# State space products in neighbouring column and row groups, and norm sums taken tile by tile, in a two-block fp32 kernel

## The chip, the cores and the metric

One NeuronCore of a Trainium2 chip. The metric is device microseconds of one execution. Of the engines, PE is TensorE (matmul), DVE VectorE, ACT ScalarE, POOL GpSimd; SP is the engine whose queue issues most DMAs. L12 is line 12 of the kernel before.

## The reference, cut to what matters

Two blocks in a row on x of 512 tokens by 1024, all in fp32; a context of 256 tokens goes into the first.

```python
# block 1 (m = the six modulation vectors, from silu(c) @ w_mod + b_mod)
hc = _modulate(ctx, g_norm1, m_c[0], m_c[1])
hx = _modulate(x, g_norm1, m_x[:, 0], m_x[:, 1])          # rms norm, * (1 + scale) + shift
x = x + m_x[:, 2] * _mixer_out(hx @ w_in, yx_lru, ...)    # RG-LRU and chunk branches, w_out
h2 = _modulate(x, g_norm2, m_x[:, 3], m_x[:, 4])
x = x + m_x[:, 5] * _conv_ffn(h2, w_up, ffn_conv_w, ffn_conv_b, w_down, rows, GRID_W)
x = _rmsnorm(x, g_final)
# block 2
h = rms_norm(x, mix_norm_g)
u, q, k, v, f_logit, g_ssm, g_att = jnp.split(h @ w_in, IN_SPLITS, axis=-1)
y_ssm = s5_branch(u, ...)              # 32 groups: x = B u, complex scan, y = Re(C s) + d u, glu
y_att = forgetting_attention(q, k, v, f_logit, ...)       # q and k normed by head
x = x + (sigmoid(g_ssm) * y_ssm + sigmoid(g_att) * y_att) @ w_out
x = x + peer_ffn(rms_norm(x, ffn_norm_g), w_query, sub_keys, peer_u, peer_v)
```

## The kernel before, in words

Activations lie transposed: 128 channels on the partitions, 8 tiles k (KT), 512 tokens (T) along the free axis; the context has 256 (TC). For fp32 accuracy every large product is three matmuls, hi by hi, hi by lo and lo by hi (mm3, L121 to 124). The halves are made by a pair of operations: ACT copies a value rounded to fp32r, DVE subtracts it from the value (weights whi and wlo, L114 and L115; activations, split_to, L142 to 145). Weights come in pieces of 512 KB over SP's queue into four raw buffers; whi and wlo have three buffers each. proj (L131) makes one column of 128 outputs from eight k, 24 matmuls, and get_w loads and splits a column's weights, once, at the first call. The build orders the instructions of each engine by a list scheduler from their readiness and their program order; every engine then runs its list in order.

Stages, in us from the span's start: opening 0 to 63; RG-LRU 63 to 302 (lru_in, lru_gates, v_cols); chunk branch, gates and w_out to 638; norm 2 to 672; conv FFN to 1026; final norms to 1062; attention with the state space between its parts to 1420; w2_glu and w2_out to 1563; norm 3 to 1590; then the expert layer (query, top 16, peer_u, peer_v) to 2891.

**Norms.** A norm over channels is a sum over the partitions and the eight k. ACT squares all eight tiles, colsum (L147) adds them in PSUM by eight matmuls against ones in four column groups of 32, ACT copies the result, and tok_mean (L154) brings it to tokens on partitions by one small matmul for each 128 tokens. rstd_of (L164) is the root (whose first use loads a table on ACT) and a reciprocal; bcast_tok (L170) spreads it over the partitions by four diagonal copies and four matmuls; scaled_split (L180) makes each normed tile (nt, hi, lo).

**Modulation.** A chapter of w_mod is 512 columns: mod_a (L203) runs eight fp32 matmuls in four column groups and copies the result, mod_b (L215) transposes it and adds the bias. Chapters 0 and 1 are the shift, 2 and 3 the scale of norm 1, 10 and 11 the factor behind the FFN.

**Opening (L237 to 285).** SP issues x, ctx and the four chapters, 2 MB each, in wm, which has two buffers. Both norms, the four chapters in order, then eight steps k of h tiles for x and for ctx; the projections of w_rx column 0 and then 1 (lru_in, L330) use them, in PSUM pool ps1 with four banks of the tag mm; ps2 has two double banks.

**Chunk branch.** v_w (L403) loads a quarter of w_v. **w_out (L674 to 677)** and **w_down (ffn_down, L793; last calls L817)** update x1 column by column; **norm 2 (L735 to 755)** has mod_a of chapters 10 and 11 in it; the **final norms (L832 to 856)** form mean1 of x1, mean2 of x1*gf and r1, r2, write x1*gf*r1 back (L854) and make hb.

**Attention and S5 (L862 to 1181).** s5_step (L1006) is put 17 times between the parts of attention. Step s runs s5_y of s-1 and s5_x of s, s from 0 to 15. s5_x (L969) has two matmuls over 32 rows, L974 real and L975 imaginary, both in row group s mod 4, into two banks, and 12 DVE operations on 128x512: six that multiply by the factors e from DRAM, two scans, four products sr, p, w2, w1. s5_y (L996) has four matmuls (L1002) of 32 output columns into column group s mod 4 of one bank, py; after each fourth step DVE adds d*u. fp32 matmuls appear as two instructions each. a_sums (L1033) sums squares of two of q, q, k, k in column groups; a_norm1 (L1035) is root and reciprocal; a_norm2 (L1041) spreads rows of rs by four matmuls (L1045), each with its own full selq and a bank of its own. All share eight banks (psD).

**w2_out (L1218 to 1221), norm 3 (L1257 to 1260)**: then rows_of_x3 (L1263) transposes token tiles of x3; the order is tile NTD = 3, 0, 1, 2.

The core of the places where the order is set by hand, before:

```python
for ch in range(4):                                   # opening
    mod_b(psp, s[ch], ch)
    if ch < 2:
        s.append(mod_a(psp, wk, ch + 2, whole=wm[ch + 2]))
def s5_step():
    s = S5["n"]
    if s > 16:
        return
    if s > 0:
        s5_y(s - 1)
    if s < 16:
        s5_x(s)
    if s < 15:
        s5_e(s + 1)
```

Of the kernel before, what the change touches and what calls it, by code (L numbers as in the profile page):

```python
# [21 lines left out]
T = 512  # L22
# [50 lines left out]
def tile_kernel(ctx: ExitStack, tc: tile.TileContext, I, out, dump=None, stop=None):  # L73
# [22 lines left out]
    c32 = const.tile([128, 2], F32, name="c32")  # L96
    nc.vector.memset(c32, 1.0 / (32 * D))
# [49 lines left out]
    def colsum(ps, sqs, n):  # L147
        K = len(sqs)
        for k in range(K):
            g = k % 4  # L150
            nc.tensor.matmul(ps[32 * g:32 * g + 32, :n], ones[:, :32], sqs[k], start=k < 4, stop=k >= K - 4)  # L151

    def tok_mean(wk, psp, sqs, n, tag):

        pa = psp.tile([128, 512], F32, name="pa", tag="mm")
        colsum(pa, sqs, n)
        s = wk.tile([128, n], F32, name="ssum", tag="ssum", bufs=1)
        nc.scalar.activation(s, pa[:, :n], AF.Copy)
        pb = psp.tile([128, 512], F32, name="pb", tag="mm")
        for t in range(n // 128):  # L160
            nc.tensor.matmul(pb[:, 2 * t:2 * t + 2], s[:, t * 128:(t + 1) * 128], c32, start=True, stop=True)
        return pb[:, 0:2 * (n // 128):2]
# [52 lines left out]
    def mod_b(psp, s, ch):  # L215
        pt = psp.tile([128, 512], F32, name="pt", tag="mm")
# [23 lines left out]
    wm = []  # L240
    for ch in range(4):
        t = wk.tile([128, 8, 512], F32, name="wm", tag="wm", bufs=2)
        for q in range(2):
            nc.sync.dma_start(t[:, 4 * q:4 * q + 4], I["w_mod"][ch][:, 4 * q:4 * q + 4])
        wm.append(t)

    def sq_of(src, n):
        s = wk.tile([128, n], F32, name="sq", tag="sq", bufs=4)
        nc.scalar.activation(s, src, AF.Square)
        return s  # L250
# [1451 lines left out]
```

## Time and profile before

| what | value |
|---|---|
| median of 3 runs | 2893.77 us (2893.13 to 2897.28) |
| profiled execution | 2892.62 us |
| its span in the profile | 2890.8 us |
| DVE, ACT, POOL busy | 73%, 40%, 17% of the span |
| HBM traffic | 186 GB/s over the span |

A row of a timeline has start and duration in us, engine, line, operation, output and inputs by the program's names, shapes and count; in brackets the idle time of the engine before it and what ended it. Durations of PE overlap, since matmuls are pipelined: what one costs is read from start to start.

### The profile page before, as it was taken

To read this page: it belongs to the slowest core of one execution; us is meant where nothing else is said; L and a number is where in the kernel's file an instruction comes from. 1 tells how busy PE (TensorE), PEld (TensorE's weight loads), DVE (VectorE), ACT (ScalarE), POOL (GpSimd) and SP (SyncE) were. 2 spreads that over 40 slices of the span, in tenths; PEclk is the share of its full clock that TensorE was granted. 3 is DMA by queue.
4 is the path that set the end of the run, shared out by engine and by line. 5 is a ranking of instruction groups with operands and counts; after the bars stand their busy time and mean duration, and the time that the engine had idled before them with its cause. 6 is when DMAs were issued, how large, how long until landed. Compare 5 with 4: busy or idle time off the path is not lost.

```text
span 2890.8 us, 37068 instructions
## 1 busy us (share of the span) xinstructions
PE 2785.8 (96%) x13917; PEld 2280.5 (79%) x13917; DVE 2099.1 (73%) x3645; ACT 1159.4 (40%) x1599; POOL 492.2 (17%) x452
## 2 busy tenths in 40 slices
PE   7999999999999999999999988999998989999999
PEld 5777888877888866656687888898998978777887
DVE  5786894339777665777544999999785579988554
ACT  4667523224333343333433334555553333333332
POOL 0000000000000000000000016546343357652000
PEclk8999999999999999999999999999999999999999
DMA  6333263333333332222233237898899699999663
GB/s 246 122 112 109 97 196 106 124 114 105 97 92 96 89 124 73 73 73 66 75 102 116 88 126 267 299 340 310 323 330 337 234 349 380 401 390 347 216 214 116
DMA packets 167476, 540.11 MB, mean 187 GB/s; under 512 B 16896, under 2 KB 42112, under 8 KB 163840
## 3 DMA queue, kind: packets, MB, share of 16 engines
q1 hardware_dynamic: 128128, 391.94, 39.7%
q0 software_dynamic: 36864, 134.23, 12.5%
q10 hardware_dynamic: 2304, 11.57, 1.1%
q8 instruction: 109, 1.79, 0.2%
q14 instruction: 71, 0.58, 0.1%
HBM read 479.48 MB, written 58.20 MB: 186 GB/s over the span
## 4 chain that ended last, share of the span: by engine, by line
PE 74%; DVE 10%; issue 6%; DMA 5%; POOL 3%; ACT 3%; SPq 0%; DVEq 0%; POOLq 0%; ACTq 0%
PE pmm L122 15%; PE pmm L124 15%; PE pmm L123 15%; PE acc L1604 13%; DMA raw<-in_peer_v_rows_dram 3%; DVE wlo L115 2%; PE pmm L1002 2%; POOL rows L1458 2%; DVE rows L1471 1%; PE pm L209 1%; PE pa L151 1%; POOL rows L1457 1%; PE pg L122 1%; PE pg L123 1%; ACT whi L114 1%
## 5 line engine op out<-in xcount | busy, mean ns | idle before, releaser
L114 ACT ACTIVATE whi<-raw 128x1024 fp32r<-128x1024 f32 (+2 forms) x502 | 518.1, 1033 | 1023.3 <-PE pmm L123 773.4
L115 DVE TENSOR_TENSOR wlo<-raw,whi 128x1024 fp32r<-128x1024 f32 (+2 forms) x502 | 608.0, 1212 | 283.5 <-ACT whi L114 278.9
L124 PE MATMUL pmm<-nph,wlo 128*128 128x384 f32 (+1 forms) x1152 | 398.9, 347 | 20.3 <-DVE wlo L115 20.2
L122 PE MATMUL pmm<-nph,whi 128*128 128x384 f32 (+1 forms) x1152 | 405.7, 352 | 0.3 <-ACT whi L114 0.3
L123 PE MATMUL pmm<-npl,whi 128*128 128x384 f32 (+1 forms) x1152 | 397.5, 345 | 0.0
L1604 PE MATMUL acc<-whi,wth 128*128 128x512 f32 x768 | 243.0, 397 | 7.3 <-ACT whi L114 7.3
L1604 PE MATMUL acc<-wlo,wth 128*128 128x512 f32 x768 | 243.6, 398 | 6.2 <-DVE wlo L115 6.1
L124 PEld LDWEIGHTS pmm<-nph,wlo 128*128 128x128 f32 x1152 | 220.3, 191 | 29.9 <-DVE wlo L115 24.8
L1604 PE MATMUL acc<-whi,wtl 128*128 128x512 f32 x768 | 242.6, 397 | 0.0
L122 PEld LDWEIGHTS pmm<-nph,whi 128*128 128x128 f32 x1152 | 220.6, 192 | 5.1 <-ACT whi L114 0.6
L123 PEld LDWEIGHTS pmm<-npl,whi 128*128 128x128 f32 x1152 | 220.4, 191 | 4.5
L1458 POOL DMA_INDIRECT rows<-in_peer_v_rows_dram,idx x128 | 202.0, 1578 | 108.5 <-DVE accN L1486 97.5
L1471 DVE SCALAR_TENSOR_TENSOR rows<-rows,hN 128x1024 f32<-128x1024 f32 x128 | 155.1, 1218 | 55.3 <-DMA rows<-in_peer_u_rows_dram,idx 55.3
L1486 DVE SCALAR_TENSOR_TENSOR accN<-rows,dot,accN 128x1024 f32<-128x1024 f32 x128 | 163.7, 1279 | 27.3 <-DMA rows<-in_peer_v_rows_dram,idx 27.0
L1604 PEld LDWEIGHTS acc<-wlo,wth 128*128 128x128 f32 x768 | 143.8, 188 | 45.8 <-DVE wlo L115 11.0
L1604 PEld LDWEIGHTS acc<-whi,wth 128*128 128x128 f32 x768 | 144.6, 189 | 44.3 <-ACT whi L114 9.2
L1604 PEld LDWEIGHTS acc<-whi,wtl 128*128 128x128 f32 x768 | 144.8, 189 | 35.8
L1458 POOL DMA_INDIRECT rows<-in_peer_u_rows_dram,idx x128 | 164.0, 1281 | 48.6 <-POOL rows L1457 26.0
L144 ACT ACTIVATE wth<-w 128x384 fp32r<-128x384 f32 x128 | 66.7, 522 | 244.0 <-PE acc L1604 223.7
L145 DVE TENSOR_TENSOR wtl<-w,wth 128x384 fp32r<-128x384 f32 x128 | 70.8, 554 | 101.9 <-ACT wth L144 101.9
L122 PE MATMUL pmm<-h2h,whi 128*128 128x512 f32 x352 | 139.2, 397 | 2.1 <-ACT h2h L186 2.0
L124 PE MATMUL pmm<-h2h,wlo 128*128 128x512 f32 x352 | 138.0, 394 | 2.8 <-DVE wlo L115 2.8
(492 smaller groups left out, 5855.8 us busy)
## 6 DMA issues: line engine op xcount, KB each, us to landing
raw<-in_peer_u_dram SPq DMA_DIRECT2D x128, 512.0 KB, 5.3
raw<-in_peer_v_rows_dram SPq DMA_DIRECT2D x128, 512.0 KB, 6.2
GD<-G SPq DMA_DIRECT2D x12, 2048.0 KB, 11.4
Gg<-GD SPq DMA_DIRECT2D x64, 384.0 KB, 8.5
raw<-in_w_up_dram SPq DMA_DIRECT2D x44, 512.0 KB, 3.5
AD<-act SPq DMA_DIRECT2D x48, 384.0 KB, 6.4
act<-AD SPq DMA_DIRECT2D x48, 384.0 KB, 7.0
raw<-in_w_mod_dram SPq DMA_DIRECT2D x32, 512.0 KB, 3.9
```

Source lines behind the costliest of these rows:

```text
L114: nc.scalar.activation(hi[:, :n], raw[:, :n], AF.Copy)
L115: (eng or nc.vector).tensor_tensor(out=lo[:, :n], in0=raw[:, :n], in1=hi[:, :n].bitcast(F32), op=OP.subtract)
L122: nc.tensor.matmul(ps, wh, ah, start=first, stop=False)
L123: nc.tensor.matmul(ps, wh, al, start=False, stop=False)
L124: nc.tensor.matmul(ps, wl, ah, start=False, stop=last)
L144: nc.scalar.activation(hi, src, AF.Copy)
L145: nc.vector.tensor_tensor(out=lo, in0=src, in1=hi.bitcast(F32), op=OP.subtract)
L1002: nc.tensor.matmul(py[32 * i:32 * i + 32], CD[c][:, s], x, start=n == 0, stop=n == 3)
L1458: nc.gpsimd.indirect_dma_start(out=r, out_offset=None, in_=I[tab], in_offset=bass.IndirectOffsetOnAxis(ap=at, axis=0))
L1471: nc.vector.scalar_tensor_tensor(r, r, 1.0, hN, op0=OP.mult, op1=OP.mult, accum_out=dot[:, n:n + 1])
L1486: nc.vector.scalar_tensor_tensor(accN, r, dot[:, n:n + 1], accN, op0=OP.mult, op1=OP.add)
L1604: nc.tensor.matmul(acc[t][q], a[:, c], bb[:, q * 512:(q + 1) * 512], start=f, stop=l)
```

## The change

- Norm sums: a class SumSq squares each tile on ACT and adds it to one accumulator on DVE or GpSimd as the tile comes; the mean is four small matmuls by 1/D. `sqrt_table()` is a one-element root, issued ahead.
- Opening: SP's order is x, ctx, chapter 2, w_rx 0 and 1, chapters 0, 3, 1. The context's adds and its products by rstd are on GpSimd. h tiles 0 to 3 come after chapters 2 and 0; the two w_rx columns run side by side, k by k, in all four banks of ps1, with chapters 3 and 1 (in ps2) between.
- v_w: the low half of one piece, column group 1, second half, on GpSimd.
- w_out: squares added by GpSimd behind each column (the last on DVE), the weights of the next column fetched ahead; chapter 10 after the last column. Chapter 11 goes to FFN step j == 2. Norm 2's tiles are interleaved with two w_up columns.
- w_down's last calls: both sums of the final norms behind each finished column; r1 and r1*r2, hb made from x1 by r1*r2*gf*mg, interleaved with two w2_u columns; x1*gf*r1 afterwards.
- S5: step s issues the imaginary input product of s and the real one of s+1; the outputs sr and p of s alternate with w2 and w1 of s-1; one step more, w1 and w2 three buffers. a_norm2: four matmuls of 32 rows each, in four row groups, issued together into four banks.
- w2_out and norm 3: as norm 2; one transposed tile ahead of norm 3's tiles, three behind.

```diff
+        def add(self, src, eng=None, scale=1.0):
+            if self.k == 0:
+                nc.scalar.activation(self.acc, src, AF.Square, scale=scale)
+            else:
+                s = self.pool.tile([128, self.n], F32, name=self.sqtag, tag=self.sqtag, bufs=self.bufs)
+                nc.scalar.activation(s, src, AF.Square, scale=scale)
+                (eng or nc.vector).tensor_tensor(out=self.acc, in0=self.acc, in1=s, op=OP.add)
+            self.k += 1
...
+    for ch in (2, 0, 3, 1):
+        wm[ch] = wk.tile([128, 8, 512], F32, name="wm", tag="wm", bufs=2)
...
+        if ch == 2:
+            rraw = [load_raw(I["w_rx"][n].rearrange("p k c -> p (k c)"), 1024) for n in range(2)]
...
+    for k in range(KT):
+        sc.add(ct[:, k], nc.gpsimd)
...
-        nc.vector.tensor_tensor(out=ct[:, k], in0=ct[:, k], in1=prc, op=OP.mult)
+        nc.gpsimd.tensor_tensor(out=ct[:, k], in0=ct[:, k], in1=prcs, op=OP.mult)
...
+    for x, ch in zip(s_, (2, 0)):
+        mod_b(psp, x, ch)
+    h_tiles(0)
+    rx_mm(0, 2)
+    s_ = [mod_a(psp, wk, ch, whole=wm[ch], wide=ps2) for ch in (3, 1)]
+    rx_mm(2, 3)
+    for x, ch in zip(s_, (3, 1)):
+        mod_b(psp, x, ch, wide=ps2)
+    h_tiles(4)
+    rx_mm(3, KT)
...
+        return load_w(I["w_v"][cv][:, 4 * q:4 * q + 4].rearrange("p k c -> p (k c)"),
+                      eng=nc.gpsimd if (cv, q) == (1, 1) else None)
...
+        get_w(*(("w_out", d + 1) if d < KT - 1 else ("w_up", 0)))
         nc.vector.scalar_tensor_tensor(x1[:, d], pp, m2h[:, d:d + 1], x1[:, d], op0=OP.mult, op1=OP.add)
+        if d == KT - 1:
+            ms = mod_a(ps, midp, 10, 1)
+            get_w("w_up", 1)
+            sqrt_table()
+        s2.add(x1[:, d], nc.gpsimd if d < KT - 1 else nc.vector)
...
+    r1 = rstd_of(const, s2.mean(psm()), T, "r1")
+    mod_b(ps, ms, 10)
...
     for k in range(KT):
         scaled_split(n2p, pr, A2[:, k:k + 1], x1[:, k], h2h[:, k], h2l[:, k], T, bias=modx[:, 24 + k:25 + k])
+        two(k, pg01, "w_up", (0, 1), h2h, h2l)
...
+        if j == 2:
+            mod_b(ps, mod_a(ps, fp, 11, 1), 11)
...
+        if k0 + kg == 22:
+            sa.add(x1[:, d], nc.gpsimd if d < KT - 1 else nc.vector)
+            sb.add(x1[:, d], scale=gf[:, d:d + 1])
...
+    for k in range(KT):
+        scaled_split(np_, pr12, gfm[:, k:k + 1], x1[:, k], hbh[:, k], hbl[:, k], T)
+        two(k, pu01, "w2_u", (0, 1), hbh, hbl)
     for k in range(KT):
         nc.vector.scalar_tensor_tensor(x1[:, k], pr1, gf[:, k:k + 1], x1[:, k], op0=OP.mult, op1=OP.mult)
-        scaled_split(np_, pr2, mg[:, k:k + 1], x1[:, k], hbh[:, k], hbl[:, k], T)
...
+    def s5_in(s, c):
 
         q, i = divmod(s, 4)
         rows = slice(32 * i, 32 * i + 32)
-        pxr, pxi = psm(), psm()
-        nc.tensor.matmul(pxr, BT[0][rows, q], uT[rows, q], start=True, stop=True)
-        nc.tensor.matmul(pxi, BT[1][rows, q], uT[rows, q], start=True, stop=True)
+        px = S5["x", s, c] = psm()
+        nc.tensor.matmul(px, BT[c][rows, q], uT[rows, q], start=True, stop=True)
+
+    def s5_x(s):
+        if s == 0:
+            s5_in(0, 0)
+        s5_in(s, 1)
+        if s < 15:
+            s5_in(s + 1, 0)
+        pxr, pxi = S5.pop(("x", s, 0)), S5.pop(("x", s, 1))
...
+        for n in range(2):
+            for u, j in ((s, n), (s - 1, 2 + n)):
+                if 0 <= u < 16:
+                    q, i = divmod(u, 4)
+                    if i == 0 and j == 0:
+                        S5["py", q] = psm()
+                    nc.tensor.matmul(S5["py", q][32 * i:32 * i + 32], CD[(0, 2, 1, 1)[j]][:, u], S5["s", u][j],
+                                     start=j == 0, stop=j == 3)
...
-        if s > 16:
+        if s > 17:
...
+        pbs = {j: psm() for j in (0, 2, 1, 3)}
+        for j, pb in pbs.items():
+            nc.tensor.matmul(pb, selq[32 * j:32 * j + 32], rs[32 * j:32 * j + 32], start=True, stop=True)
         for j in (0, 2, 1, 3):
-            pb = psm()
-            nc.tensor.matmul(pb, selq[j], rs, start=True, stop=True)
+            pb = pbs.pop(j)
...
-    for t in (NTD, *range(NTD)):
+    rows_of_x3(NTD)
+    pr = bcast_tok(n3, ps, r3, T)
+    for k in range(KT):
+        scaled_split(n3, pr, P("ffn_g", k), x3[:, k], nph[:, k], npl[:, k], T)
+    for t in range(NTD):
         rows_of_x3(t)
```

## Rows read from the trace of the kernel before

**Rows 1.** The page, section 1: busy time, share and instructions of each engine.
```profile
PE 2785.8 (96%) x13917; PEld 2280.5 (79%) x13917; DVE 2099.1 (73%) x3645; ACT 1159.4 (40%) x1599; POOL 492.2 (17%) x452
```

**Rows 2.** Windows: length; PE, PEld, DVE, ACT, POOL busy (instructions); PEclk, DMA, GB/s.
```profile
0.00:63.00 63.00, 48.44 (x252) 30.11 (x256) 33.59 (x108) 25.16 (x51) 0.78 (x11) 0.84 0.63 246
...
1062.00:1420.00 358.00, 358.00 (x1599) 229.84 (x1598) 251.78 (x392) 137.29 (x246) 0.00 (x0) 0.99 0.23 74
```

**Rows 3.** Timeline of PE, 0 to 64: start, duration, instruction, idle before.
```profile
24.40 1.07 PE L209 MATMUL pm<-wm,cz 128*32 128x512 f32 x8
...
36.94 1.94 PE L209 MATMUL pm<-wm,cz 128*32 128x512 f32 x8
...
43.21 0.80 PE L122 MATMUL px<-hxh,whi 128*128 128x512 f32 x1 [1.70 <-ACT hxh L144]
...
62.64 0.27 PE L124 MATMUL pc<-hch,wlo 128*128 128x256 f32 x1
```

**Rows 4.** DMA view, 0 to 64 us: what the 16 engines moved in 40 slices.
```profile
GB/s 0 244 384 420 430 415 435 435 425 420 420 435 282 5 51 246 415 430 425 425 430 405 420 407 271 18 0 0 207 143 248 108 256 20 0 10 0 0 0 0
```

**Rows 5.** Timeline of DVE, 36 to 64: two h tiles in a row.
```profile
57.08 0.54 DVE L279 TENSOR_SCALAR nt<-xt,A,modx 128x512 f32<-128x512 f32 x1
...
59.26 0.54 DVE L279 TENSOR_SCALAR nt<-xt,A,modx 128x512 f32<-128x512 f32 x1
```

**Rows 6.** Groups of instructions on POOL: busy and mean ns, idle before.
```profile
L1373 POOL TENSOR_TENSOR eq<-eq,idf 128x1024 f32<-128x1024 f32 x12 | 36.2, 3021 | 26.1 <-DVE eq L1371 26.1
```

**Rows 7.** Timelines of ACT and PE, 270 to 290.
```profile
274.94 1.05 ACT L114 ACTIVATE whi<-raw 128x1024 fp32r<-128x1024 f32 x1
...
282.88 0.45 PE L420 MATMUL pv<-wlo,hxh 128*128 128x256 f32 x1 [4.76 <-DVE wlo L115]
```

**Rows 8.** Timelines of DVE, PE and ACT, 636 to 673, in order of time.
```profile
638.18 0.75 DVE L677 SCALAR_TENSOR_TENSOR x<-pmm,m2h,x 128x512 f32<-128x512 f32 x1 [4.69 <-PE pmm L124]
...
643.40 1.05 PE L209 MATMUL pm<-raw,cz 128*32 128x512 f32 x4 [3.41 <-DMA raw<-in_w_mod_dram]
...
649.62 1.05 PE L161 MATMUL pb<-c,ssum 128*128 128x2 f32 x8
...
650.34 1.28 ACT L166 ACT_TABLE_LOAD   x1
...
654.70 1.41 DVE L182 SCALAR_TENSOR_TENSOR nt<-pr,A,x 128x512 f32<-128x512 f32 x2
```

**Rows 9.** Timeline of DVE, 1025 to 1063.
```profile
1026.97 0.75 DVE L793 SCALAR_TENSOR_TENSOR x<-pmm,modx,x 128x512 f32<-128x512 f32 x1 [2.69 <-PE pmm L124]
...
1042.85 1.41 DVE L182 SCALAR_TENSOR_TENSOR nt<-pr,par,x 128x512 f32<-128x512 f32 x2 [0.24 <-PE pr L177]
```

**Rows 10.** Timeline of DVE, 1562 to 1591.
```profile
1563.76 0.69 DVE L1221 SCALAR_TENSOR_TENSOR x<-pmm,x 128x512 f32<-128x512 f32 x1 [3.40 <-PE pmm L124]
...
1574.18 1.41 DVE L182 SCALAR_TENSOR_TENSOR nt<-pr,par,x 128x512 f32<-128x512 f32 x2 [1.01 <-PE pr L177]
```

**Rows 11.** Timeline of PE, 1220 to 1232: N, Y, X, and what follows.
```profile
1221.12 3.60 PE L1045 MATMUL pmm<-rs,selq 128*128 128x512 f32 x8
1224.65 1.04 PE L1002 MATMUL pmm<-sr,CD 128*32 128x512 f32 x2
...
1228.20 1.12 PE L974 MATMUL pmm<-uT,BT 32*128 32x512 f32 x2
...
1230.11 0.50 PE L122 MATMUL pmm<-qh 128*128 128x512 f32 x1
```

**Rows 12.** Timeline of PE, 1195 to 1197: two S matmuls (a_sums) and the next instruction.
```profile
1195.06 1.05 PE L1033 MATMUL pmm<-qs,ones 128*32 128x512 f32 x4
1196.05 0.50 PE L122 MATMUL pmm<-hbh,whi 128*128 128x512 f32 x1
```

**Rows 13.** Timeline of PE, 1201 to 1206: a step of the state space in parts.
```profile
1202.68 1.12 PE L974 MATMUL pmm<-uT,BT 32*128 32x512 f32 x2
1203.74 1.04 PE L1002 MATMUL pmm<-p,CD 128*32 128x512 f32 x2
```

More of the change, by code (lines that the diff above doesn't have):

```diff
@@ L95, in tile_kernel @@
     nc.vector.memset(ones, 1.0)
[L96 to L97 removed]
+    cD = const.tile([128, 2], F32, name="cD")
+    nc.vector.memset(cD, 1.0 / D)
+    junk = const.tile([128, 1], F32, name="junk")
     epsb = const.tile([128, 1], F32, name="epsb")
@@ L145, in split_to, with __init__, mean, sqrt_table @@
         nc.vector.tensor_tensor(out=lo, in0=src, in1=hi.bitcast(F32), op=OP.subtract)
[L147 to L162, printed above, removed]
+    class SumSq:
+        def __init__(self, pool, n, tag, sqtag="sq", bufs=2, acc=None):
+            self.pool, self.n, self.sqtag, self.bufs, self.k = pool, n, sqtag, bufs, 0
+            self.acc = pool.tile([128, n], F32, name=tag, tag=tag, bufs=1) if acc is None else acc
+        def add(self, src, eng=None, scale=1.0):
[6 more added lines that the diff above has]
+            self.k += 1
+        def mean(self, pb):
+            for t in range(self.n // 128):
+                nc.tensor.matmul(pb[:, 2 * t:2 * t + 2], self.acc[:, t * 128:(t + 1) * 128], cD, start=True, stop=True)
+            return pb[:, 0:2 * (self.n // 128):2]
+    def sqrt_table():
+        nc.scalar.activation(junk, epsb, AF.Sqrt)
     def rstd_of(wk, mean, n, tag):
@@ L239, in tile_kernel @@
     nc.sync.dma_start(ct, I["ctx"])
-    wm = []
-    for ch in range(4):
-        t = wk.tile([128, 8, 512], F32, name="wm", tag="wm", bufs=2)
+    wm = {}
+    rraw = []
+    for ch in (2, 0, 3, 1):
+        wm[ch] = wk.tile([128, 8, 512], F32, name="wm", tag="wm", bufs=2)
         for q in range(2):
[L244 to L250, printed above, removed]
@@ L256, in tile_kernel @@
+    for k in range(KT):
+        sx.add(xt[:, k])
+    rx = rstd_of(wk, sx.mean(psp.tile([128, 512], F32, name="pb", tag="mm")), T, "rx")
+    s_ = [mod_a(psp, wk, 2, whole=wm[2])]
+    for k in range(KT):
+        sc.add(ct[:, k], nc.gpsimd)
     prx = bcast_tok(wk, psp, rx, T)
+    rc = rstd_of(wk, sc.mean(psp.tile([128, 512], F32, name="pb", tag="mm")), TC, "rc")
     prc = bcast_tok(wk, psp, rc, TC)
+    prcs = wk.tile([128, TC], F32, name="prcs", tag="sqc", bufs=2)
+    nc.scalar.activation(prcs, prc, AF.Copy)
@@ L763, in ffn_g @@
     def ffn_g(j):
-        pg = psm()
-        proj(pg, "w_up", j, *h2)
+        if j < 2:
+            pg = pg01[j]
+        else:
+            pg = psm()
+            proj(pg, "w_up", j, *h2)
         pad = pads[j % NP]
@@ L1176, in tile_kernel @@
             s5_step()
-    while S5["n"] <= 16:
+    while S5["n"] <= 17:
         s5_step()
```

177 lines of the change are left out of this document (96 added, 81 removed).

## The prediction

> **What bounds the kernel now.** I read the page's busy line, then busy time by stage, then timelines of the six places that the change touches. TensorE (PE) is busy for 96% of the span [rows 1], so a gain must take PE work away, let matmuls overlap, or fill PE's gaps. By stage [rows 2]: in attention (1062 to 1420) PE is busy for all 358.00 us and DVE for 251.78, so only fewer or overlapping matmuls help there; in the opening (0 to 63) PE is busy 48.44 us at a mean clock of 0.84. The other places are seams, where PE stands while a norm's statistics come together.
>
> The profiled execution took 2892.62 us, its span 2890.8 and 1.8 around it; that is 1.15 below the median of 2893.77. Gains are summed against it and carried to the median.
>
> **Opening: gain 12.** Four chapters of modulation come first, in order; from the last one's matmuls at 36.94 the chain to the first projection at 43.21 (copy, transposing matmuls, first h tile, its split) takes 6.3 us, and the block of two projections ends at 62.64 [rows 3]. After the change two chapters are enough to begin. The DMA row (slices of 1.6 us) shows some 420 GB/s up to the 13th slice, 7.6 MB by 20.8 us, then two slices of nothing, since wm has two buffers [rows 4]. In the new order 1 MB of w_rx goes ahead of the second chapter on SP's queue, so that this chapter has landed after 8.6 MB, near 23 us. With 6.3 behind it the first projection starts near 29. DVE then paces: it starts one k after the other each 2.18 us [rows 5], 17.5 for eight. The two late chapters and their transposes cost PE some 2 to 6 more (half a chapter takes 1.07 at 24.40 and 1.94 at 36.94, which is the low one of PE's two clocks), part of it under DVE's pace. The end comes at 48 to 53 instead of 62.8: I take 12, and keep 7 to 16. Where they could queue: two columns now hold all four banks of the first PSUM pool, so the late chapters use the second pool, which is empty; SP stands behind the wait for chapter 2's buffer before it can issue chapters 3 and 1, and the w_rx and w_lru loads behind these are wanted only after 48. The sums of squares leave PE for ACT and 7 adds on DVE, at a time when DVE has only x to wait for. GpSimd gets 7 adds and 8 products of 128x256 for the context; its nearest row, 3021 ns for 128x1024 [rows 6], makes an estimated 0.76 of each, 11 us in all, from about 10 to 25. They cost nothing while the modulation is awaited; without that cover the context tiles would be late by their part, some 5 us.
>
> Rows 5 show DVE without GpSimd beside it. The Trainium skill (SBUF — State Buffer, "Who interferes with whom") says that a DVE instruction with two inputs in SBUF contends with a GpSimd one that reads SBUF. That speaks against the change; no row of this kernel bears on it, and it is rival 4's rule.
>
> **One low half on GpSimd: gain 5.** PE waits 4.76 us at 282.88 for a wlo whose high half was there by 276.0 [rows 7]; DVE had scans to do first. On GpSimd it takes 3.02 [rows 6], so it ends at 279 at the latest. PE was free at 278.1, so the wait shrinks to 1 at most. The matmuls behind it run slow (the first, of 256 columns, takes 0.45; the one at 62.64 [rows 3], also of 256, 0.27), which I put at 1 more. Next late is the following wlo, still DVE's. 3 to 6.5.
>
> **Norm 2: gain 10.** After the last w_out matmul PE waits 3.41 for a chapter's DMA; sums follow, and from the mean's matmuls at 649.62 to the first h2 tile at 654.70 it is 5.1 us, 1.28 of it a table load [rows 8]. With squares added as each column is done, the chain behind the last update (638.18 + 0.75) is a square and an add, each about as long as that update, 1.4, and the same way from mean to tile without the load, 3.8: the tile starts near 644. The load moves ahead of the last square: it may cost its 1.28 there. Chapter 10 stands in the same place (2.9 of PE) and its DMA may be as late as before (3.41). Chapter 11 leaves the seam, its four DMAs past the first w_up loads on SP, and costs PE its 3 us later, in the FFN, where nothing hides it. So 10.5 earlier, 3 paid back, and an estimated 2.5 because each tile now feeds two columns at once, 1.4 us of PE beside 1.41 of DVE for its product and split: 10; 5 if the DMA is late, 14 at best. GpSimd's adds, about 1.5 each (half of 3.02), lie beside the 5.5 us of matmuls of the next column; without that cover one of them is exposed.
>
> **Final norms: gain 9.5.** Between the last update, which ends at 1027.7, and the first hb tile at 1042.85 two norms follow one another [rows 9]. After: square and add 1.4, mean to tile 3.8 as in norm 2, and 1 for the second root and its small steps: the tile at 1033.9, 9 earlier; half a us more comes from two columns per tile. The eight products by gf, as long as the tile's own (1.41 for two), stood between the tiles; 5.6 us of DVE, they go behind them and under matmuls, and without that cover they would be the next late thing. 5 to 11, as DVE's tiles may pace the two columns.
>
> **Norm 3: gain 5.** The last update starts at 1563.76 and takes 0.69, the first tile starts at 1574.18 [rows 10]. By 1.4 and 3.8 as above it is at 1569.7, 4.5 earlier; of the four tile transposes that stand ahead of the projections one stays: 5 in all. 3 to 8. What follows shifts with it.
>
> **Attention: gain 41.** From start to start [rows 11] four N matmuls (norm of q and k) take 3.53, four Y (state space output) 3.55, so 0.89 each, and two X (its input) 1.91, so 0.955. In all 16 N are 14.1, 64 Y 57, 32 X 30.6. Overlap is seen on column groups only: two S matmuls in 0.99 [rows 12], four of a chapter in 1.07 [rows 3]. Y becomes 30 pairs at 0.99 and 4 singles: 33.3, saves 23.9. X becomes 15 pairs and 2 singles: 16.8 if row groups do as column groups do, saves 13.8. N becomes four times 1.07, saves 9.8. Sum 47.5. Off it: where X stands between two parts of Y [rows 13], as in 4 of 16 steps, a pair may be torn and cost one more slot, 3.6; and 3 for waits, as a pair needs the tiles of two steps, one bank of X is held over a step, N takes four banks at once, and behind a waiting X or N stand all projections of the stage. DVE's work stays: 70% of the stage now, 80% after. Row groups are unseen: X is bounded by 0 and 13.8, N by -1.2 (four quarter-height matmuls in turn at 0.955) and 9.8. I take the upper ends, nearest to the column groups' rows. Y is at least 16, if a third of its pairs are torn. So 15 to 47.5.
>
> The Trainium skill (TensorE: Matmul & The Clock Gate, "Measured speedup vs the span model") has four row groups at 3.07 times one: N would be 14.1/3.07 = 4.6, an estimate, and the sum 0.3 less than by the row of 1.07. No run here shows it yet.
>
> **Sum.** 12 + 5 + 10 + 9.5 + 5 + 41 = 82.5; 2892.6 - 82.5 = 2810.1, or 2811 on the median. All upper ends: 16 + 6.5 + 14 + 11 + 8 + 47.5 = 103, 2791. All lower ends: 7 + 3 + 5 + 5 + 3 + 15 = 38, 2856.
>
> **Rivals.**
> 1. *Row groups run one after the other*: X and N give nothing, 82.5 - 23.6 = 59, 2835. For it: no row shows two at once; X and X stand 0.955 apart. Against: these used the same row group.
> 2. *The change does not do what it says*: instructions are ordered by readiness, and pairs come apart as in rows 13. If Y and X keep 12 and N 6, attention gives 18, the sum is 59.5, 2834. Against: 12 of 16 steps stand together now.
> 3. *Seams stay*: DVE's tiles or a DMA (the 3.41, the 2.18 pace) set their length. If opening and norms give 15 instead of 36.5: 61, 2833.
> 4. *GpSimd holds DVE* for its 11 us in the opening and 3 in the chunk branch: 82.5 - 14 = 68.5, 2825. Against: much of it falls where DVE waits.
> 5. *Slower*: each of 18 steps has X or N wait until DVE has freed banks. A step has 12 operations on DVE at a mean of 0.64 (251.78 over 392 [rows 2]), 7.7 us. If PE stands through all of them, 18 x 7.7 = 139 are lost, 56 more than the gain: 2950. It decides from 82.5/18 = 4.6 us a step. Against: X finds its banks free now, and of eight it takes one more.
>
> **Chances.** Forecast 0.59 (own range 2796 to 2826), rivals 1 and 2 0.12 each, rival 3 0.09, rival 4 0.05, rival 5 0.03. The range of 8 in 10 begins at 2789, beside the sum of upper ends, and ends at 2848, 13 past rivals 1 to 3 for the open sizes that come with them. About 0.2%, 5.8 us, can be told from no change. All cases but the fifth are 58 us or more faster: faster 0.95, same 0.02 for what lies between the lower ends and rival 5, slower 0.03.
>
> **What would show it.** Right: a first projection near 29 us; no 4.76 wait near 270; the first tile 9 to 11 us nearer to the last matmul in norm 2 and the final norms, 5 in norm 3; an X pair within 1.0, N's four within 1.1, Y pairs within 1.0, the stage in 317 us. Wrong: X pairs at 1.9 or N's four at 3.5 (rival 1), single Y or X in many steps (2), tiles as far from the last matmul as before (3), DVE operations that grow beside GpSimd (4), waits of PE for DVE of more than 5 us in attention (5).

## The result and the profile after

After: 2850.10 us, median of 4 runs (2847.70 to 2852.82), against 2893.45 (2890.18 to 2897.28) of before on the same chip: 0.9843 of it, 95% interval 0.9828 to 0.9858. The gain is 43 us where 82.5 were forecast, and the time lies 2 us above the range. The profiled execution took 2852.11, its span 2850.3, so 40.5 less than that of before. Lines L are those of the kernel after from here on.

The stretches below run from one first or last matmul of TensorE to the next; they were read from the timelines and add up to the span. "Again" is a second trace of the kernel after (e12_after_again), which shows how much one stretch differs by itself.

| stretch, ends with | before | after | again | gain | forecast |
|---|---|---|---|---|---|
| opening and RG-LRU: last px product | 200.1 | 196.4 | 196.7 | 3.8 | 12 |
| chunk branch: last pv product | 101.0 | 102.6 | 100.8 | -1.6 | 5 |
| to the last w_out product | 336.6 | 337.9 | 337.9 | -1.3 | 0 |
| norm 2, FFN: last w_down product | 388.8 | 385.6 | 385.4 | 3.2 | 10 |
| final norms: first X | 35.9 | 29.3 | 28.2 | 6.6 | 9.5 |
| attention: first w2_out product | 457.0 | 429.2 | 429.3 | 27.7 | 41 |
| norm 3: first product with the keys | 70.7 | 66.7 | 66.3 | 4.1 | 5 |
| expert layer: end | 1300.7 | 1302.7 | 1297.0 | -2.0 | 0 |

No stretch gave what was forecast, and attention and opening hold most of the shortfall, 13 and 8 of 42 us.

How much a stretch differs by itself shows in the runs below, which each leave most of the code alone. Over all traces with the code of after in a stretch, the opening with RG-LRU takes 196.4 to 198.7 us, the chunk branch 100.8 to 102.8, norm 2 with the FFN 384.1 to 386.1, the final norms 28.0 to 30.9, norm 3 66.3 to 68.3, and the expert layer, which no run touches, 1296.0 to 1306.8; attention keeps within 429.0 to 429.3. e1_attention_only, which is before everywhere but in attention, differs from before by 1.4 us in the opening, 2.1 in the FFN and 1.6 in norm 3. Outside attention a difference of 1 or 2 us between two traces shows nothing yet.

The busy line of the page and busy time by stage:

```profile
PE 2733.1 (96%) x13821; PEld 2263.9 (79%) x13821; DVE 2111.3 (74%) x3657; ACT 1157.6 (41%) x1597; POOL 542.3 (19%) x486
```

```profile
0.00:60.00 60.00, 42.56 (x228) 27.43 (x232) 39.44 (x111) 28.11 (x55) 13.46 (x26) 0.91 0.66 258
1051.80:1481.00 429.20, 417.28 (x2045) 295.45 (x2045) 294.95 (x461) 172.85 (x305) 0.00 (x0) 0.99 0.27 89
```

Against [rows 1, 2], PE has lost work, but it is no longer busy all through attention: 417.28 of 429.20 us. GpSimd works 13.46 us in the opening.

**Attention.** PE's timeline, the pieces that answer to [rows 11 to 13]:

```profile
1072.59 1.13 PE L1045 MATMUL pmm<-uT,BT 32*128 32x512 f32 x4
1073.64 0.39 PE L1010 MATMUL pmm<-fl,tri 128*128 128x8 f32 x2
...
1116.88 1.14 PE L1132 MATMUL pmm<-rs,selq 32*128 32x512 f32 x8
1117.95 0.62 PE L1085 MATMUL pmm<-sr,CD 128*32 128x512 f32 x1
...
1156.22 1.90 PE L1085 MATMUL pmm<-w,CD 128*32 128x512 f32 x4
...
1218.66 0.62 PE L1085 MATMUL pmm<-sr,CD 128*32 128x512 f32 x1
1218.66 0.62 PE L1085 MATMUL pmm<-w,CD 128*32 128x512 f32 x1
```

From start to start two X of neighbouring row groups take 1.05 us, four N 1.07; two Y of neighbouring column groups start together (a step's two pairs take 1.8). At 1156.22 w2 and w1 of a step stand alone, without the sr and p of the next step: three of the steps are torn like this and cost 1.8 more each. Over the stage X fell from 31.3 to 17.8, N from 14.1 to 4.3, Y without its waits from 57.3 to 38.2: 42 us less. What was given back is PE's waits there, 1.05 us before, 11.9 now:

```profile
PE pmm L1085 <- DVE p L1059: 2.3, 3, 1.3
PE pmm L123 <- ACT qh L145: 1.9, 2, 1.5
PE pmm L123 <- ACT ph L145: 1.6, 2, 0.8
PE pmm L124 <- DVE ql L146: 1.1, 2, 0.6
PE pmm L123 <- DVE w L1059: 1.1, 1, 1.1
PE pmm L1186 <- ACT pp L1178: 1.0, 1, 1.0
```

(Waits of PE by line and by whom, with total, times, longest.) The six rows hold 9.0 of the 11.9 us. They are many small waits, for q and k (qh, ql), the softmax (pp, ph) and the state space tiles (p, w); none stands before an X or an N.

**Opening.** DVE's timeline:

```profile
44.59 0.16 DVE L229 TENSOR_TENSOR modx<-pg,par 128x4 f32<-128x4 f32 x1 [5.02 <-PE pg L227]
...
47.99 0.16 DVE L229 TENSOR_TENSOR modx<-pg,par 128x4 f32<-128x4 f32 x1 [2.97 <-PE pg L227]
...
48.19 0.55 DVE L291 TENSOR_SCALAR nt<-xt,A,modx 128x512 f32<-128x512 f32 x1
```

and PE's:

```profile
20.90 0.61 PE L167 MATMUL pb<-cD,sc 128*128 128x2 f32 x4 [1.82 <-POOL sc L161]
21.44 1.15 PE L218 MATMUL pm<-wm,cz 128*32 128x512 f32 x8
...
31.81 0.80 PE L123 MATMUL px<-hxh,whi 128*128 128x512 f32 x1
...
38.34 1.92 PE L218 MATMUL pg<-wm,cz 128*32 128x512 f32 x14
...
45.05 1.06 PE L218 MATMUL pg<-wm,cz 128*32 128x512 f32 x8
...
59.01 1.92 PE L218 MATMUL pm<-raw,cz 128*32 128x512 f32 x16
```

The first projection comes at 31.81 (43.21 in [rows 3]), but from there to chapter 4's matmuls, which close the block, it is 27.2 us instead of 19.6 (26.6 to 28.1 over all traces with this opening, with first projections at 31.7 to 34.8): the late chapters' matmuls and transposes lie between products, DVE stands 7.99 us for them, and the second four tiles start at 48.19.

**Chunk branch.** PE's timeline of the second trace, whose clock is like that of before here:

```profile
262.97 0.39 PE L460 MATMUL pv<-wlo,hxh 128*128 128x256 f32 x1 [1.71 <-POOL wlo L116]
279.44 0.58 PE L460 MATMUL pv<-wlo,hxh 128*128 128x256 f32 x1 [4.69 <-DVE wlo L116]
```

The wait of 4.76 us [rows 7] is still there, for DVE, as 4.69 us (3.21 in the first trace of after, whose stretch is the longer one all the same); the piece that went to GpSimd is an earlier one, which had been waited for 0.52 us in before.

**Norm 2 and FFN.** The first products with a tile of norm 2, before and then after:

```profile
656.25 1.65 PE L122 MATMUL pmm<-h2h,whi 128*128 128x512 f32 x3 [1.98 <-ACT h2h L186]
```

```profile
646.81 1.65 PE L123 MATMUL pmm<-h2h,whi 128*128 128x512 f32 x3 [1.60 <-ACT h2h L195]
```

They start 9.9 us after the last w_out product (636.91), against 18.5 (637.75), and the first two columns of w_up are done 9.6 us earlier relative to it. From there to the last w_down product it takes 6.4 us more than before.

### The profile page after: what moved, and what is told of

Same layout as the page of the kernel before. It is cut to its first block, busy times and chain, and to the rows that moved or that the text cites. A ratio compares the mean times of both kernels' runs of the same rounds, so it can differ in the third digit from the quotient of the medians.

```text
span 2850.3 us, 36948 instructions
## 1 busy us (share of the span) xinstructions
PE 2733.1 (96%) x13821; PEld 2263.9 (79%) x13821; DVE 2111.3 (74%) x3657; ACT 1157.6 (41%) x1597; POOL 542.3 (19%) x486
## 4 chain that ended last, share of the span: by engine, by line
PE 69%; DVE 13%; issue 7%; DMA 4%; POOL 4%; ACT 2%; DVEq 0%; POOLq 0%; SPq 0%; ACTq 0%
PE pmm L123 15%; PE pmm L124 15%; PE pmm L125 15%; PE acc L1699 14%; DMA raw<-in_peer_v_rows_dram 3%; DVE wlo L116 3%; POOL rows L1553 2%; DVE rows L1566 1%; POOL rows L1552 1%; PE pmm L1085 1%; ACT whi L115 1%; PE pg L123 1%; PE pg L124 1%; PE pg L125 1%; PE pm L218 1%
## 5 line engine op out<-in xcount | busy, mean ns | idle before, releaser
L1581 DVE SCALAR_TENSOR_TENSOR accN<-rows,dot,accN 128x1024 f32<-128x1024 f32 x128 | 163.7, 1279 | 27.9 <-DMA rows<-in_peer_v_rows_dram,idx 27.7
L1699 PEld LDWEIGHTS acc<-wlo,wth 128*128 128x128 f32 x768 | 144.2, 189 | 46.5 <-DVE wlo L116 12.5
```

Source lines behind the costliest of these rows:

```text
L1581: nc.vector.scalar_tensor_tensor(accN, r, dot[:, n:n + 1], accN, op0=OP.mult, op1=OP.add)
L1699: nc.tensor.matmul(acc[t][q], a[:, c], bb[:, q * 512:(q + 1) * 512], start=f, stop=l)
```

## The experiments

All ran beside the kernel before; the ratio is to its runs on the same chip.

| run | median us | ratio and interval |
|---|---|---|
| e1_attention_only | 2865.58 | 0.9894, 0.9869 to 0.9919 |
| e2_pairs_kept | 2848.45 | 0.9838, 0.9813 to 0.9863 |
| e3_opening_order | 2850.2 | 0.9835, 0.9808 to 0.9861 |
| e4_other_piece | 2853.52 | 0.9844, 0.9812 to 0.9875 |
| e5_right_piece | 2847.25 | 0.9829, 0.9805 to 0.9852 |
| e6_no_reciprocal | 2854.07 | 0.9858, 0.9841 to 0.9874 |
| e7_context_on_dve | 2849.78 | 0.9840, 0.9823 to 0.9856 |
| e8_chapter11_in_seam | 2846.37 | 0.9831, 0.9815 to 0.9848 |
| e9_chapters_first | 2847.79 | 0.9840, 0.9824 to 0.9857 |
| e10_steps_spread | 2851.93 | 0.9858, 0.9841 to 0.9874 |
| e11_combined | 2838.34 | 0.9824, 0.9801 to 0.9847 |
| e12_after_again | 2848.33 | 0.9853, 0.9832 to 0.9875 |

The intervals of the runs e2 to e12 overlap one another, so single edits are judged by their own stretch in the trace.

**e1_attention_only**: the kernel before with the state space and a_norm2 of after, nothing else.

> The kernel before with the attention part of the change alone (paired inputs and outputs of the state space, four norm matmuls in four row groups). Theory A, the parts add up: the attention stage shortens by the 27.7 us that it did in the changed kernel, X by 13.6, N by 9.8 and Y by 14, and new waits of PE for DVE of about 11 us appear; total 2893 - 28 = 2865. Theory B, the stages lean on one another (the earlier start of the projections in the changed kernel made the waits): waits under 4 us and a gain of 34 or more, total below 2860.

The stage took 428.3 us instead of 457.0, X and N gave the same 13.5 and 9.8, and PE's waits were 11.97. So attention's gain and its waits are the change's own, and not a consequence of the other parts.

**e2_pairs_kept**: what completes a pair may not go ahead of its first half.

```diff
-                    nc.tensor.matmul(S5["py", q][32 * i:32 * i + 32], CD[(0, 2, 1, 1)[j]][:, u], S5["s", u][j],
-                                     start=j == 0, stop=j == 3)
+                    with (tc.issue_after(first.ins) if j >= 2 and s < 16 else ExitStack()):
+                        m = nc.tensor.matmul(S5["py", q][32 * i:32 * i + 32], CD[(0, 2, 1, 1)[j]][:, u], S5["s", u][j],
+                                             start=j == 0, stop=j == 3)
+                    if j < 2:
+                        first = m
```

> The changed kernel with w2 and w1 of the step before queued on PE behind sr and p of this step, so that no pair of Y comes apart. Theory A, the three torn steps cost 1.8 us each on PE: 5.4 us less, total 2845, Y (64 matmuls) at 37 to 38 us instead of 43.1. Theory B, DVE paces the state space, so PE waits instead for sr and p: Y's matmuls shrink but waits of PE for DVE grow by as much, total within 2 us of the changed kernel's 2850.

No step is torn, Y takes 36.9 us with its waits instead of 43.1, and the waits grow to 14.2; the stage is 425.9, 3.3 shorter. The torn pairs cost 6 by themselves and half of that on the path.

**e3_opening_order**: PE's order kept as written, chapters 3 and 1 and their transposes behind two k.

```diff
+    order.enter_context(tc.manual_schedule(engines={mybir.EngineType.PE}))
...
     rx_mm(0, 2)
     s_ = [mod_a(psp, wk, ch, whole=wm[ch], wide=ps2) for ch in (3, 1)]
-    rx_mm(2, 3)
     for x, ch in zip(s_, (3, 1)):
         mod_b(psp, x, ch, wide=ps2)
     h_tiles(4)
-    rx_mm(3, KT)
+    rx_mm(2, KT)
```

> The changed kernel with PE's order in the opening written out: chapter 2 whole ahead of the context's mean, chapters 3 and 1 and their transposes straight behind the products of k 0 and 1. Theory A, PE's order held the chapters back (chapter 2's second half behind the context's mean, chapter 1's transposes behind products of k 2 and 3): the second four h tiles start near 41 instead of 48.2 us, the two columns end near 53 instead of 59, total 2850 - 6 = 2844. Theory B, the chapters' transfers set it: start of the second four tiles moves by less than 2 us and the total stays within 2 us.

DVE's waits for the chapters:

```profile
42.95 0.16 DVE L229 TENSOR_TENSOR modx<-pg,par 128x4 f32<-128x4 f32 x1 [3.18 <-PE pg L227]
...
44.38 0.16 DVE L229 TENSOR_TENSOR modx<-pg,par 128x4 f32<-128x4 f32 x1 [1.01 <-PE pg L227]
```

They fell to 4.19 us and the second four tiles began at 44.58, 3.6 earlier; the block ended at 56.99, only 2.0 earlier, and 24.8 us after its first projection (32.20). The first theory has the direction, but its 41 and 53 were missed by some 4 us.

**e9_chapters_first**: the same, with the chapters behind one k (rx_mm(0, 1), then rx_mm(1, KT)).

> The kernel after with TensorE's order of the opening kept as written, and with the matmuls and transposes of chapters 3 and 1 behind the products of the first k alone (in e3_opening_order they came behind the first two, and in the kernel after between those of k 2 and 3). Theory A (in the kernel after VectorE stands 7.99 us for the transposes of these two chapters, 5.02 and 2.97 us; both could be done while TensorE waits for tiles anyway): VectorE starts the second four tiles at 40 to 42 us instead of 48.19 us, the matmuls of chapter 4, which close the block, start at 54 to 55.5 us instead of 59.01 us (56.99 us in e3_opening_order), and the last px product comes 3.5 to 5 us before 196.38 us. What is left then is TensorE's own work: eight products of 2.1 us, two chapters of 3.6 us together and their transposes, 22.5 us from the first projection on, so that the forecast end of 50.8 us could not be had from a first projection at 31.8 us. Rival (the chapters' weights arrive too late for this place, or TensorE does them at its low clock): TensorE waits for the weights in front of the chapter's matmuls or they take over 6 us, and the block ends at 57 us or later.

PE's timeline; of the products only the first behind the chapters is shown:

```profile
36.01 4.35 PE L218 MATMUL pg<-wm,cz 128*32 128x512 f32 x32
40.29 1.05 PE L227 MATMUL pg<-sel,ms 128*128 128x2 f32 x8
41.76 1.02 PE L227 MATMUL pg<-sel,ms 128*128 128x2 f32 x8 [0.42 <-DVE A L288]
42.65 0.48 PE L123 MATMUL px<-hxh,whi 128*128 128x512 f32 x1
...
57.50 1.92 PE L218 MATMUL pm<-raw,cz 128*32 128x512 f32 x16
```

The tiles were no longer late (DVE went on at 42.82), and yet the block ended at 57.50, no earlier than in e3. From 42.65 PE runs seven k without a wait, 2.1 us each. Here my theory of the run missed by 2 us or more: the first k took 4.4 us (31.58 to 36.01) and the chapters 4.35 instead of 3.64. But it shows the bound: once the order is mended, PE's own work fills the block.

**e7_context_on_dve**: the context's adds and products on DVE.

```diff
-        sc.add(ct[:, k], nc.gpsimd)
+        sc.add(ct[:, k])
...
-        nc.gpsimd.tensor_tensor(out=ct[:, k], in0=ct[:, k], in1=prcs, op=OP.mult)
+        nc.vector.tensor_tensor(out=ct[:, k], in0=ct[:, k], in1=prcs, op=OP.mult)
```

> The kernel after with the squares' sums and the products of the context on VectorE instead of GpSimd. Theory A (in the opening, GpSimd's slow sum delays the context's mean, the second half of chapter 2 behind it on TensorE, and through the weight buffer the load of chapter 1; and GpSimd and VectorE hold each other): the mean at 20.90 us comes 1 to 2 us earlier, the four dg operations of VectorE go back from 1.88 us to about 0.9 us, and the second four tiles start 1 to 3 us earlier than 48.19 us. Rival (VectorE has no room for this work before the first product): the first projection comes later than 31.81 us by 1 to 3 us, and the second four tiles start no earlier than 48 us.

```profile
24.50 1.06 PE L218 MATMUL pm<-wm,cz 128*32 128x512 f32 x8 [0.62 <-DMA wm<-in_w_mod_dram]
```

The mean came at 19.18, 1.7 earlier, and chapter 0's second half ran at 24.50 as soon as its DMA was in. But DVE now had fifteen operations of 0.4 us more to do, the first projection came at 31.57, 0.2 earlier, and the second four tiles at 48.02. Both placements cost about the same: the theory held for the early part and fell for the end.

**e4_other_piece** and **e5_right_piece**: another low half of w_v on GpSimd.

```diff
-                      eng=nc.gpsimd if (cv, q) == (1, 1) else None)
+                      eng=nc.gpsimd if (cv, q) == (2, 1) else None)
```

(In e4 it is (2, 0).)

> The changed kernel with another quarter's low half on GpSimd: the first half of column group 2 instead of the second half of column group 1. Theory A, the change moved a piece whose wait was 0.5 us and left the piece with the long wait on DVE: the wait of 3.2 us near 277 falls to under 1, the one of 1.7 near 262 goes back to 0.5, total 4 us less, 2846. Theory B, any piece on GpSimd costs as much as it saves, as DVE and GpSimd hold each other up: the sum of the two waits stays above 4 us, total within 2 us.

Its long wait stayed, 4.77 us at 283.34, and that of 1.70 fell to 0.52: (2, 0) had slack too, so it was the wrong piece again; the wait of 4.7 us belongs to (2, 1), as e5 shows.

> The kernel after, but with the low half of the second half of w_v's third piece on GpSimd, instead of the second half of the second piece. In the kernel after the third piece's second half still waits 3.21 us for VectorE's low half (product at 280.74), and the moved piece waits 1.70 us for GpSimd (264.26), where before it waited 0.52 us. Theory A (the change moved the wrong piece; the step was otherwise sound): the wait of 3.21 us falls below 1 us and the one of 1.70 us goes back to about 0.5 us, the stretch from the last px product to the last pv product, 102.6 us in the kernel after, comes to 98 to 100 us, and the run is 3 to 4 us below the kernel after, about 2846 to 2847 us. Rival (GpSimd is too slow for any piece, or VectorE is held by it): the wait stays at 2 us or more under GpSimd's name, and the stretch stays at 102 to 103 us.

PE's waits of e5:

```profile
263.55 0.39 PE L460 MATMUL pv<-wlo,hxh 128*128 128x256 f32 x1 [0.52 <-DVE wlo L116]
269.95 0.39 PE L459 MATMUL pv<-whi,hxh 128*128 128x256 f32 x1 [0.86 <-ACT v L462]
274.65 0.39 PE L460 MATMUL pv<-wlo,hxh 128*128 128x256 f32 x1 [1.68 <-POOL wlo L116]
288.16 0.38 PE L460 MATMUL pv<-wlo,hxh 128*128 128x256 f32 x1 [1.97 <-DVE wlo L116]
```

The wait of 4.7 became 1.68, for GpSimd's 2.84 us; but one of 0.86 came back and one of 1.97 is new, for the next low halves, which DVE makes behind its scans. The stretch took 99.0 us, and 100.2 in e11_combined, which has the same piece; the nine traces with after's piece took 100.8 to 102.8. The right piece was worth about 2 us, not 5.

**e8_chapter11_in_seam**: mod_a of chapter 11 directly behind the broadcast of norm 2, mod_b behind its tiles, nothing of it in the FFN.

```diff
     pr = bcast_tok(n2p, ps, r1, T)
     pg01 = [psm(), psm()]
+    m11 = mod_a(ps, n2p, 11, 1)
...
+    mod_b(ps, m11, 11)
     get_w("w_up", 22)
...
-        if j == 2:
-            mod_b(ps, mod_a(ps, fp, 11, 1), 11)
```

> The kernel after with chapter 11's modulation begun in the seam of norm 2, right behind the broadcast of the norm, instead of after the second h2 tile of the FFN. Theory A (in the kernel after, chapter 11's matmuls stand on TensorE's path in the FFN and cost about 3.6 us there, against nothing in the seam, where TensorE waits for the tiles): from the two columns done to the last h2 tile it is 320 to 321 us instead of 324.4 us, the seam of norm 2 keeps its length to within 1 us, and the run is 2 to 4 us below the kernel after. Rival (the seam's gaps are too short or the tiles come later): the seam gets longer by 2 to 4 us, and the sum of the two stretches stays the same within 1 us.

```profile
643.42 1.55 PE L186 MATMUL pr<-dg,ones 128*128 128x128 f32 x8 [1.69 <-DVE dg L185]
644.90 2.68 PE L218 MATMUL pm<-raw,cz 128*32 128x512 f32 x8
647.52 0.74 PE L123 MATMUL pmm<-h2h,whi 128*128 128x512 f32 x2
648.66 1.05 PE L218 MATMUL pm<-raw,cz 128*32 128x512 f32 x4
```

Half of the chapter lies where PE had waited 1.60 us for the first tile. The seam (up to the two columns done) is 2.1 us longer than in after, the FFN from there to the last w_up product 4.6 shorter (319.8 against 324.4), together 2.5 less; against the second trace of after it is 1.0 and 3.4, together 2.4. That lies between the two theories.

**e6_no_reciprocal**: a_norm1 without nc.vector.reciprocal(rs, rs).

> The kernel after without VectorE's reciprocal over 1024 columns in the norm within the attention stage (four of 3.3 us): the products are then made with the root instead of its reciprocal, so this part of the computation is left out. Theory A (VectorE's row of work, 76% busy there, sets the waits of TensorE that take back what the products gave): TensorE's waits in the attention stage, 11.9 us in the kernel after, fall by 5 to 11 us, and the stage, 429.2 us, comes to 418 to 424 us. Rival (the waits come from the order of the items and the latency of each chain, not from VectorE's amount of work): the waits stay within 2 us of 11.9 us, and the stage stays at 427 to 431 us.

Busy time up to the last Y, after and then e6:

```profile
1051.80:1366.90 315.10, 306.31 (x1544) 208.41 (x1544) 240.19 (x385) 125.26 (x224) 0.00 (x0) 0.99 0.26 84
```

```profile
1054.00:1369.00 315.00, 306.18 (x1544) 208.34 (x1544) 227.67 (x381) 124.91 (x224) 0.00 (x0) 0.99 0.26 84
```

DVE has 12.5 us less to do and PE has gained nothing: waits 11.95, stage 429.3. The theory that DVE's amount of work sets the waits falls, as far as 5% of this work can tell.

**e10_steps_spread**: three state space steps moved to the last pair of heads.

```diff
             a_sums(pa, raw, (0, 1))
-        s5_step()
+        if i == 3:
+            s5_step()
         a_pv(2 * i, pT, v_, g0)
```

> The kernel after with three of the 18 state space steps moved later: none between the transposes and the value products of the first head of the first three pairs of heads, and instead three steps in the last pair of heads, which in the kernel after has none. Nothing is computed otherwise. Theory A (TensorE's new waits in the attention stage, 11.9 us, come from what is put between the two ends of a chain on ScalarE and VectorE: the state space steps that lay there got shorter by 2.5 us each, and steps that follow closely wait for their own tiles): the waits of the last pair of heads, 2.9 us in the kernel after, go, the others change by less than they, and the sum of waits is 8 us or less, the stage 426 us or less. Rival (the waits are as many wherever the steps are put): the sum stays between 10.5 and 14 us and the stage between 428 and 432 us.

PE's waits (the first two rows) and two stretches of busy time:

```profile
PE pmm L1186 <- ACT pp L1178: 1.9, 1, 1.9
PE pmm L124 <- DVE ql L146: 1.9, 3, 0.6
```

```profile
1260.00:1300.00 40.00, 39.25 (x203) 27.42 (x203) 29.88 (x47) 16.70 (x33) 0.00 (x0) 0.87 0.25 79
...
1350.00:1400.00 50.00, 46.92 (x218) 27.84 (x216) 34.56 (x55) 21.43 (x45) 0.00 (x0) 0.93 0.20 63
```

The sum of waits fell to 7.8, as the theory of the order has it, but the stage took 429.9, as the rival has it: the columns of the granted clock, 0.87 and 0.93, stand for some 17 us at the low one of the two levels (13% of 40 us and 7% of 50, each twice), where the whole stage of after stands at 0.99. So where the steps stand does bear on the waits, and PE lost at the low clock what it had won: with 4.1 us less of waits, its instructions at the two low places took an estimated 7 us more than the same ones take on average in after. Why the clock fell there stays open.

**e11_combined** and **e12_after_again**: the edits of e2, e3, e5 and e8 together, and the kernel after.

> The kernel after with the four edits that gained a stretch by themselves: the state space pairs kept together (e2_pairs_kept), the order of the opening (e3_opening_order), the right half of w_v on GpSimd (e5_right_piece) and chapter 11 in the seam of norm 2 (e8_chapter11_in_seam). Theory A (the four places lie one behind the other, so what they gave in their own stretches adds: 2.0 to the last px product, 3.6 to the last pv product, 2.5 in the seam of norm 2 with the FFN, 3.3 in the attention stage, 11.4 us in all): a median some 11 us below that of the kernel after on the same chip, about 2839 us where that has 2850. Rival (TensorE, given fewer waits, runs more of its time at its low clock, as the steps spread out in e10_steps_spread had 4.1 us less of waits and no shorter stage): 3 to 6 us below it.

> The kernel after itself, on the same chip and in the same rounds as e11_combined. Both theories: 0.983 to 0.986 of the kernel before, and the waits of TensorE in the attention stage and the order of its instructions the same as in the first trace of the kernel after, so that what the stretches differ by between two traces of one kernel is what TensorE's low clock does.

2838.34 against 2848.33 us, 10.0 less, near the 11.4 of the sum; the intervals of the two ratios overlap. By stretches: 162.0 instead of 165.0 from the first to the last px product, 100.2 instead of 100.8 in the chunk branch, 344.4 instead of 346.8 from the last w_out to the last w_up product, 425.9 instead of 429.3 in attention, but 1.3 more in the final norms and 6.8 more in the expert layer (1303.9 against 1297.0), so that the two profiled executions themselves are alike, 2843.93 and 2843.40 us. e11 has the lowest median and ratio of all versions; that the four gains add up in the total is likely, and not shown beyond the noise.

## Why the prediction was wrong, step by step

**Direction and overlap held.** Rival 1 falls: row groups overlap, X gave 13.5 of 13.8, N 9.8 of 9.8. Rival 2 holds for three steps of fifteen, where the forecast had four; but a torn step costs 1.8 us and not the 0.9 that it was priced at. The rule behind N (the Trainium skill, TensorE: Matmul & The Clock Gate, "Measured speedup vs the span model") gave an estimate of 4.6 us; 4.3 were measured, so the trace agrees. Rival 3 does not hold, though it names the direction of the shortfall: the first tile came nearer to the last matmul by 8.6 us in norm 2, 6.0 to 7.3 in the final norms and 3.6 in norm 3, less than the 10.5, 9 and 4.5 of the sums. Rival 5's sign came, as 7.0 us of PE's waits in attention are for DVE and the forecast named 5; its mechanism and price did not, with no wait before an X or an N, and 11.9 us of waits instead of 139.

**Attention, 27.7 instead of 41.** The products gave 42 of the 43.9 that were left after the torn pairs (of Y, 57 less 33.3 is 23.7 and not 23.9, which changes nothing). The step that failed is "3 for waits": 10.9 were added, and some 4 more lie in instructions that took longer, 2.0 of it in the transposes of pp and 0.9 in the products of yh behind the attention parts (more of these under norm 2). I had looked for waits at the banks that X and N need, and at DVE's share. e6 shows that 12.5 us less work on DVE change nothing, e10 that the place of the steps is part of it. The reading that fits is this: a state space step between two parts of attention had hidden the way of the softmax and of q and k through ACT and DVE, and a step is now some 2.5 us shorter. That the waits are for these tiles is in the rows; that the shorter steps uncovered them is argued, and no run shows it by itself. The forecast never asked what the removed time had been hiding.

**Opening, 3.8 instead of 12.** Two steps failed. The first projection came at 31.8 instead of 29: its chapter had landed at 24.50 (e7's row) and not near 23, and in after PE came to that half only at 26.82, behind the context's late mean. And the rest took 27.2 us instead of 21.8. "DVE then paces ... 17.5 for eight", with the chapters in part under that pace, was wrong: by e9 a k costs PE 2.1 us, so of DVE's 2.18 only 0.6 us in all eight were free, and products, chapters (3.6) and transposes (2) are 22.5 us of PE's own. The order added its part: DVE stood 7.99 us. e3 and e9 got back 2.0 and 1.5 of 8.2 us against the first trace of after. Part of it ran at the low clock (0.91 in the opening's row), but that is not what made it long: in e4 and e6 the granted clock is 1.00 from 0 to 60 us, and the block still takes 26.7 and 26.6 us from its first projection. With first projections at 31.6 to 33.2 no order that was tried ended before 56.99.

**GpSimd and DVE hold each other** (rival 4, 0.05). DVE's rows in the opening, the same operation with GpSimd's products beside it and later without:

```profile
29.15 0.69 DVE L287 SCALAR_TENSOR_TENSOR A1c<-modc,par 128x4 f32<-128x4 f32 x1
...
30.74 0.81 DVE L291 TENSOR_SCALAR nt<-ct,A1c,modc 128x256 f32<-128x256 f32 x1
31.52 1.17 DVE L146 TENSOR_TENSOR hxl<-nt,hxh 128x512 fp32r<-128x512 f32 x1
...
34.17 0.69 DVE L146 TENSOR_TENSOR hxl<-nt,hxh 128x512 fp32r<-128x512 f32 x1 [0.37 <-ACT hxh L145]
...
44.87 0.16 DVE L287 SCALAR_TENSOR_TENSOR A1c<-modc,par 128x4 f32<-128x4 f32 x1
```

0.69 against 0.16, 1.17 against 0.69, around the first projection; in e7, without GpSimd's work, they take 0.15 and 0.69 there too. With the rule (the Trainium skill, SBUF — State Buffer, "Who interferes with whom") both agree, as they read two inputs in SBUF. Not each such operation was held: the one for A at 29.07 took 0.17. With the four diagonal copies at 15.83 (1.88 us, in before 0.88) DVE lost an estimated 2.4 us, not the 14 of the rival, and without it (e7) DVE has the same time to work itself.

**Chunk branch, nothing instead of 5.** The step had the right wait and the wrong piece: the 4.76 us belong to the third piece's second half, and the diff moves the second's. And "next late is the following wlo" was left unpriced: e5 shows 1.97 us of it, so that even the right piece gives about 2.

**Norm 2, 3.2 instead of 10.** The seam and two columns gave 9.6 (8.5 in the second trace) of the 13 that stood for them before the 3 for chapter 11. Paid back are 6.4: about 3.6 for chapter 11, and w_down's products, which the forecast had at their old price. PE's group of one of the three products in the FFN, after and before:

```profile
L124 PE MATMUL pmm<-fl,whi 128*128 128x512 f32 x175 | 69.3, 396 | 0.0
```

```profile
L123 PE MATMUL pmm<-fl,whi 128*128 128x512 f32 x175 | 68.0, 389 | 0.0
```

They start 0.234 instead of 0.229 us apart, in all kernels with the new FFN and not in e1_attention_only: 2.4 us over 528. Products of the branches ahead of w_out do the same (most of the -1.3 there). In attention the products of yh do it too, and e1, whose yh keep 0.229, has a stage 0.9 us shorter. The cause wasn't tried and stays open.

**Final norms and norm 3** had sizes too high: 6.6 to 7.7 of 9.5, 4.1 to 4.4 of 5 (over all traces with this code 5.0 to 7.8 and 2.5 to 4.4). `sqrt_table()` did nothing at its places: ACT's view of its line shows all three one-element roots at the start of the program,

```profile
L171 ACT ACTIVATE junk<-epsb x3: 202/203/203, 2.0 to 2.5; 128x1 f32<-128x1 f32 x3
```

since they depend on nothing and the list scheduler takes them first. The loads of 1.28 us stayed in front of the real roots, and cost little there, as they lie under the last add and the mean's matmuls. ACT's root of norm 3, behind its load:

```profile
1530.11 0.26 ACT L175 ACTIVATE r<-pmm,epsb 128x4 f32<-128x4 f32 x1 [1.12 <-PE pmm L167]
```

In the final norms it waits 0.37 us for the mean, and only in norm 2 does it follow its load at once.

**Sum.** Short by 13 in attention, 8 in the opening, 7 each in the chunk branch and in norm 2 with the FFN, 3 in the final norms, 1 in norm 3, and 3 in stretches that I had at nothing, of which the last differs by 5.7 us between two traces of one kernel. Three terms came out below their own lower ends (opening 7, chunk branch 3, norm 2 5), attention's was taken near its upper end, and the range of the sum did not hold them all falling short together.

## What to carry to other kernels

When matmuls get shorter, list what they had been covering before booking the gain: a third of what the overlap gave (15 of 42 us) went back into waits of 0.2 to 1.5 us each and into instructions that took longer. Price a moved block on every engine that works beside it (PE's 2.1 us beside DVE's 2.18), and tie a wait to its piece by the buffer's turn before moving one. A preload without a dependence on what precedes it is no preload at that place under a list scheduler.

## What the runs showed of the hardware that I had not expected

Four fp32 matmuls over 32 rows each, in four row groups, take 1.07 us together and two take 1.05, as long as one alone (1.06 in [rows 13]); two column groups give 0.9 for a pair. A DVE operation of 128x4 with both inputs in SBUF took 0.69 instead of 0.16 us beside GpSimd (the one before it 0.17), and a TENSOR_SCALAR of 128x256 0.81 instead of 0.40, though it has only one large input. GpSimd's subtraction for one low half of 128x1024 took 2.36 to 2.84 us.
